# A kernel that plans its own order: norm weights copied inside SBUF for the last tokens, a two-regime transfer model, and a table of priority shifts

## The chip, the cores and the metric

The program runs on the 8 cores of one Trainium2 chip. Each core does one batch element, and no core talks to another. The metric is the device time of the slowest core, in microseconds. Before the change it was 1097.69 us (median of 3 runs).

## The reference, cut to what matters

One layer of a decoder: 16 meta tokens and 2048 tokens of width 1024 per core. A LayerNorm is applied first. Two attention branches (latent attention "MLA" and forgetting attention "FoX") follow, then gates, a merge, a second norm, a gated feed-forward with a short convolution, and a third norm.

```python
h = layer_norm(concat([meta, x]), ln_emb_g, ln_emb_b)           # 2064 tokens
m = hybrid_mixer(h, ...)                                        # two attentions, gates, merge
h = layer_norm(ALPHA * h + m, ln_mix_g, ln_mix_b)
f = conv_glu_ffn(h, ...)
h = layer_norm(ALPHA * h + f, ln_ffn_g, ln_ffn_b)
```

2064 tokens are 16 tiles of 128 and a rest of 16. The kernel spreads the rest over all partitions: four blocks of 32 rows, each with 256 of the 1024 columns. So the weights of the norms are needed in that form too.

## The kernel before

The kernel does not fix its order by hand. Its Python code records every operation as an item. A list scheduler (called the planner below) then simulates all engines with a table of durations. At each moment it starts, on each engine, the ready item of the lowest priority number. The resulting order of each engine is emitted; semaphores, not the planned times, make each operation wait for what it needs. The part that models a transfer:

```python
    RATE = 250.0                                    # bytes per ns
    LAND = {"sp": 2000.0, "pool": 2300.0}           # ns from the last byte to the semaphore
    ...
    def _prio(self, e, prio):
        b = prio if prio is not None else self.base.get(e, self.base.get("", 0.0))
        return b * 1e6 + len(self.items)
    ...
            if it.dma is not None:
                ...
                bus[0] = max(st + (1450.0 if e == "sp" else 1900.0), bus[0]) + it.bytes / self.RATE + 20.0
                end = bus[0] + self.LAND[e]
```

The loads for the last 16 tokens, called twice: in the first stage near 124 us, and before the second norm near 638 us.

```python
        def short_load(q, xb, pk, after):
            p4 = pk[:, :].rearrange("p (a n) -> p a n", a=4)
            for j in range(4):
                J, C = slice(32 * j, 32 * j + 32), slice(256 * j, 256 * j + 256)
                K.dma(q, xb[J, 0:256], xm[L - 32:L, C], after=after)
                K.dma(q, p4[J, :, :], lnp[0:4, C].partition_broadcast(32), after=after)
            K.dma(q, xb[:, 512:640], d_rep, after=after)
            return p4
```

The first norm's weights are already in SBUF, copied to all 128 partitions (`GBe`).

```python
        wfk = at(136832, 8 * 512).rearrange("p (k n) -> p k n", k=8)      # FoX key weights
        GBe = at(136832, 2048, F32).rearrange("p (a n) -> p a n", a=2)    # first norm's weights
```

Background copies ("paced") turn the branch weights `w_c` and the feed-forward weights `w_u` into bf16, HBM to HBM. The planner issues them from 50 us on, one after another, where its model of the queue has room. Many operands are transposed by DMA, SBUF to SBUF (`flip`), not by TensorE. The SBUF tensor is one array, so the profile names these transfers and the copies that the change adds both `SB<-SB`; the operation (DMA_TRANSPOSE or DMA_DIRECT2D) tells them apart where it is shown.

The softmax here doesn't subtract the row's maximum and nothing guards it: scores larger than these inputs give would overflow.

## Time and profile before

The page of the slowest core (core 2), busy time by engine and the chain that ended last. Columns of the first line: busy us, share of the span, instructions.

```profile
span 1095.9 us, 25665 instructions; the slowest of 8 cores (1089.0 to 1095.9 us)
...
PE 1061.2 (97%) x8230; PEld 602.7 (55%) x8316; DVE 744.7 (68%) x1674; ACT 619.9 (57%) x1362; POOL 178.9 (16%) x258
...
PE 88%; DMA 3%; issue 2%; ACT 2%; DVE 2%; POOL 1%; SPq 0%; DVEq 0%; POOLq 0%; ACTq 0%
```

TensorE (PE) is busy 97% of the time and is 88% of the chain, so what can be gained lies in TensorE's gaps and in work that is only filler: the kernel issues 200 dummy matmuls that fill TensorE's waits, nearly all before 50 us. The spans of the cores, with granted clock:

```profile
core 1: 1089.0 us, clock 0.995
core 2: 1095.9 us, clock 0.993
...
core 5: 1089.6 us, clock 0.993
...
die 0 (median of its cores): 1093.3 us, clock 0.994
die 1 (median of its cores): 1091.0 us, clock 0.994
```

The cores differ by 7 us at almost equal clocks, with the same program.

### The profile page before, as it was taken

How to read it: one execution, taken by the hardware profiler on the slowest of the kernel's cores; microseconds unless marked ns; L12 is line 12 of the kernel's file. 1: busy time of each engine (PE TensorE's matmuls, PEld its weight loads, DVE VectorE, ACT ScalarE, POOL GpSimd, SP SyncE). 2: the span in 40 equal slices, each digit the busy share in tenths (PEclk: the TensorE clock that was granted, in tenths of full speed). 3: DMA queues.
4: the chain of work that ended last, by engine and by line, in shares of the span. 5: the costliest groups of instructions: out<-in, count | busy, mean ns of one | idle time of the engine just before them, and what ended most of it. 6: DMA issues, size and time to landing. Idle time of an engine off the chain costs nothing.

```text
span 1095.9 us, 25665 instructions; the slowest of 8 cores (1089.0 to 1095.9 us)
## 1 busy us (share of the span) xinstructions
PE 1061.2 (97%) x8230; PEld 602.7 (55%) x8316; DVE 744.7 (68%) x1674; ACT 619.9 (57%) x1362; POOL 178.9 (16%) x258
## 2 busy tenths in 40 slices
PE   9999889999999999999999999999999999999995
PEld 6655556667454555565555566554456664444443
DVE  3899866764566676766668887656576765667754
ACT  5789879999778888887873254431034431023300
POOL 5434221121111220302111111101100000110010
PEclk9999999999999999999999999999999999999998
DMA  8858865754677797886989386962242232234301
GB/s 174 206 106 137 146 76 78 137 81 62 156 160 174 123 226 215 148 250 128 226 213 281 98 239 158 257 162 96 99 154 97 97 105 73 112 127 151 107 20 58
DMA packets 86867, 156.54 MB, mean 143 GB/s; under 512 B 39073, under 2 KB 43121, under 8 KB 86737
## 3 DMA queue, kind: packets, MB, share of 16 engines
q1 hardware_dynamic: 70066, 123.78, 38.4%
q0 software_dynamic: 16672, 31.11, 21.3%
q8 instruction: 72, 1.18, 0.5%
q14 instruction: 57, 0.47, 0.2%
HBM read 160.38 MB, written 34.67 MB: 178 GB/s over the span
## 4 chain that ended last, share of the span: by engine, by line
PE 88%; DMA 3%; issue 2%; ACT 2%; DVE 2%; POOL 1%; SPq 0%; DVEq 0%; POOLq 0%; ACTq 0%
PE PS L187 88%; ACT SB L187 2%; DVE SB L187 2%; DMA SB<-SB 2%; DMA SB<-scr_c 1%; POOL SB L187 1%; SPq L190 0%; ACT L187 0%; DVEq L226 0%; POOLq L226 0%; DVEq L245 0%; POOL scr_c L190 0%; POOL SB L190 0%; ACTq L245 0%; SPq L245 0%
## 5 line engine op out<-in xcount | busy, mean ns | idle before, releaser
L187 PE MATMUL PS<-SB 128*128 128x65 bf16 (+11 forms) x8230 | 1061.2, 291 | 22.5 <-DVE SB L187 6.7
L187 PEld LDWEIGHTS PS<-SB 128*128 128x128 bf16 (+2 forms) x8316 | 602.7, 98 | 480.7 <-issue 88.4
L187 ACT ACTIVATE SB<-PS,SB 128x384 bf16<-128x384 f32 (+9 forms) x611 | 315.3, 582 | 250.8 <-PE PS L187 243.9
L187 ACT ACTIVATE SB<-PS 128x384 bf16<-128x384 f32 (+11 forms) x547 | 215.3, 537 | 28.5 <-PE PS L187 24.5
L187 DVE SCALAR_TENSOR_TENSOR SB<-SB 128x1024 f32<-128x1024 f32 (+7 forms) x188 | 177.4, 948 | 14.6 <-POOL SB L187 7.1
L187 ACT ACTIVATE SB<-SB 128x384 f32<-128x384 f32 (+4 forms) x153 | 97.7, 645 | 141.4 <-DVE SB L187 141.1
L187 DVE SCALAR_TENSOR_TENSOR SB<-SB,PS 128x512 f32<-128x512 f32 (+3 forms) x146 | 90.2, 620 | 118.2 <-PE PS L187 93.7
L187 DVE SCALAR_TENSOR_TENSOR SB<-PS,SB 128x384 f32<-128x384 f32 (+1 forms) x220 | 141.0, 642 | 31.9 <-ACT SB L187 23.1
L187 POOL TENSOR_TENSOR SB<-SB 128x1 f32<-128x1 f32 (+1 forms) x67 | 81.8, 1222 | 434.1 <-DVE SB L187 433.6
L187 DVE TENSOR_TENSOR SB<-PS,SB 128x384 bf16<-128x384 f32 (+10 forms) x229 | 108.6, 480 | 61.1 <-ACT SB L187 53.7
L187 DVE TENSOR_TENSOR SB<-SB 128x128 bf16<-128x128 bf16 (+7 forms) x353 | 84.7, 268 | 31.2 <-ACT SB L187 23.7
L190 POOL DMA_DIRECT2D scr_u<-w_u x88 | 44.5, 506 | 266.9 <-ACT SB L187 261.7
L187 DVE CAST SB<-PS 128x512 bf16<-128x512 f32 (+5 forms) x85 | 50.6, 599 | 23.1 <-PE PS L187 18.5
L187 DVE BATCH_NORM_STATS2 SB<-SB 128x6 f32<-128x512 f32 (+1 forms) x85 | 56.9, 675 | 4.6
L187 DVE COPY SB<-SB 32x384 bf16<-32x384 bf16 (+2 forms) x80 | 19.7, 260 | 14.1 <-PE PS L187 12.5
L190 POOL DMA_DIRECT2D scr_c<-w_c x32 | 16.6, 520 | 64.6 <-ACT SB L187 62.7
L187 DVE COPY SB<-PS 128x2 f32<-128x2 f32 (+9 forms) x66 | 19.7, 306 | 8.1 <-PE PS L187 7.7
L190 POOL DMA_DIRECT2D SB<-w_dn x22 | 11.9, 541 | 78.4 <-ACT SB L187 78.4
L187 DVE TENSOR_SCALAR SB<-SB 128x1 f32<-128x1 f32 (+2 forms) x68 | 10.3, 152 | 18.7 <-ACT SB L187 15.9
L187 DVE RECIPROCAL SB<-PS 128x3 f32<-128x3 f32 (+3 forms) x84 | 14.1, 173 | 12.6 <-PE PS L187 11.2
L187 DVE TENSOR_SCALAR SB<-PS,SB 128x128 bf16<-128x128 f32 (+1 forms) x21 | 9.5, 461 | 1.4 <-POOL SB L187 1.0
L187 DVE BATCH_NORM_AGGREGATE SB<-SB 128x2 f32<-128x12 f32 (+2 forms) x43 | 8.6, 203 | 2.4
(20 smaller groups left out, 38.9 us busy)
## 6 DMA issues: line engine op xcount, KB each, us to landing
SB<-scr_u SPq DMA_DIRECT2D x66, 512.0 KB, 3.9
SB<-scr_c SPq DMA_DIRECT2D x80, 384.0 KB, 5.3
SB<-xm SPq DMA_DIRECT2D x31, 512.0 KB, 6.8
scr_u<-w_u POOLq DMA_DIRECT2D x88, 128.0 KB, 4.0
scr_h<-SB SPq DMA_DIRECT2D x16, 512.0 KB, 4.9
SB<-scr_h SPq DMA_DIRECT2D x16, 512.0 KB, 3.5
out<-SB SPq DMA_DIRECT2D x15, 512.0 KB, 2.6
scr_c<-w_c POOLq DMA_DIRECT2D x32, 192.0 KB, 4.2
```

Source lines behind the costliest of these rows:

```text
L187: return self._add(eng, lambda e: getattr(e, name)(*args, **kw), rd, wr)
L190: return self._add(eng, lambda e: e.dma_start(out=out, in_=in_, **kw), [in_], [out], dma_key=key, after=after)
```

## The change

Its intent: replace eight broadcast reads from HBM by copies inside SBUF; give the planner a second regime of transfer times from 56 us on, with faster rate and earlier landing; and shift the priorities of each of 215 parts of the recording by a table, one number for TensorE and one for all other engines. The numbers look like the result of a search.

```diff
+    LATER = 56.0
+    RATE2 = 290.0
+    LAND2 = {"sp": 1000.0, "pool": 1200.0}
...
     def _prio(self, e, prio):
         b = prio if prio is not None else self.base.get(e, self.base.get("", 0.0))
-        return b * 1e6 + len(self.items)
+        k = self.part + (self.line != self.of or self.part < 0)
+        return b * 1e6 + len(self.items) + (RAISED[k][e != "pe"] if k < len(RAISED) else 0)
...
-                bus[0] = max(st + (1450.0 if e == "sp" else 1900.0), bus[0]) + it.bytes / self.RATE + 20.0
-                end = bus[0] + self.LAND[e]
+                late = st >= 1e3 * self.LATER
+                bus[0] = max(st + (1450.0 if e == "sp" else 1900.0), bus[0]) + it.bytes / (self.RATE2 if late else self.RATE) + 20.0
+                end = bus[0] + (self.LAND2 if late else self.LAND)[e]
...
+RAISED = ((-13118, -36714), (-8248, 20214), (9486, 14943), (22487, 38948),   ... 215 pairs, cut
...
-        def short_load(q, xb, pk, after):
+        def short_load(q, xb, pk, after, gains):
...
-                K.dma(q, p4[J, :, :], lnp[0:4, C].partition_broadcast(32), after=after)
+                for a, g in enumerate(gains):
+                    K.dma(q, p4[J, 2 * a:2 * a + 2, :], g[J, :, C], after=after)
...                                  # first stage: gains = (GBe,); second norm: gains = (GB0, GBm)
```

(`self.part` counts the parts as items are recorded; those lines are cut.)

## The prediction

> **What bounds it now.** The table of busy time by engine gives TensorE 97% (1061 of 1095.9 us); the chain of waits is 88% matmuls. From 740 to about 1075 us (feed-forward) TensorE has no gap: one 512-column matmul every 216 to 219 ns. [...]
>
> A new order can recover part of the dummies' time (DVE is already busy 16 to 19.8 of every 20 us from 20 to 120 us), part of the larger gaps, and what the slowest core loses beyond the others. Cores span 1089.0 to 1095.9 us at equal clocks; core 2 also waits for SBUF-to-SBUF transposes (8.15 us on its chain to 136 us, 6.7 us to 159 us) and one load near 608 us, costing TensorE 0.7 + 2.0 + 2.7 + 1.3 us.
>
> **What the change does.**
> 1. Copies for the last tile. Removed: 8 broadcast reads of 128 KB, 6.1 us (first norm, issued at 124 us) to 9.3 us (at 638 us) to landing. Added: 4 + 8 copies of 64 KB inside SBUF, four more issues at 0.43 us of SyncE. None is in this trace; estimate 3 to 6 us to landing, from 6.1 us for the 64 KB constant load. At 638 us TensorE is full: worth 0. At 124 us the four issues (2.4 us) stand in the chain just before a transpose; their count stays: 0 to 1.5 us gained.
> 2. Transfer model: from 56 us the planner believes in landings about 1 us earlier and rate 290 instead of 250. The 512 KB loads land in 3.9 us by the DMA list, near that; transposes take 5.4 us, later. Only order changes: -1 to +3 us.
> 3. Priority shifts, mean 0.02, at most 0.1, against 0.005 per token tile: four tiles of reordering on average. Matmul work is unchanged. Filled gaps and earlier real work: 4 to 14 us gained, before about 300 us.
>
> **Prediction.** 1089 us, range 1079 to 1098. Chances: faster by over 2% 0.05, within 2% 0.92, slower by over 2% 0.03.
>
> **What would show it.** Right: matmul counts by form unchanged; the feed-forward stretch as long as before (within 1 us) but starting 5 to 12 us earlier; gaps over 200 ns before 300 us shrink; the score bursts keep their short gaps; the broadcast loads leave the DMA list, and TensorE waits for none of the new copies. Wrong on item 1: undoing the copies alone costs over 2 us. Wrong on item 2: undoing the model alone is faster, or TensorE gains waits on loads after 56 us.
>
> **What would make it wrong.** The shifts mix attention with dense filler so well that the short burst gaps vanish (then 1070 or below), or real work replaces most dummies; or the optimistic model makes loads late, several waits of 2 us each (about 1100); or the slowest core's DMA luck moves by its 7 us.

My sum for core 1 came to about 1075 us up to the last matmul (1029 of matmuls, 46 of gaps), and about 9 us after it. Its matmul times, and with them the split of the gaps, rested on a spacing that was not measured here, so "1070 or below" in the last paragraph is only an estimate of mine; the 9 us are not shown either. What the trace of core 1 shows: the matmuls run from 1.5 to 1076.8 us, and 12.2 us follow. From start to start a 512-column matmul takes 215 to 216 ns. The 200 dummies (256 columns) take 109 ns each in the median, about 22 us in all, and start before 44 us. The short gaps of the score bursts are seen in the 64-row pairs of 384 columns: after a pair the next one starts 169 to 170 ns later, but what follows the last pair of a burst 255 ns later (44 times). The larger gaps, over 200 ns and before 300 us, come to 8.3 to 12.0 us (six cores). The forecast: the middles of its three items (0.75 gained, 1 lost, 9 gained) take 1097.7 us to 1089.

## More of the kernel before

Core 1 has a record without missing matmuls, so I read details from it. What TensorE waited for on core 1 from 60 to 165 us (us in total, times, longest):

```profile
PE PS L187 <- ACT SB L187: 2.2, 6, 1.0
PE PS L187 <- DVE SB L187: 1.2, 2, 0.9
PE PS L187 <- DMA SB<-SB: 0.4, 2, 0.2
```

Stretches of core 1 (busy time and count for PE, PEld, DVE, ACT, POOL; then granted clock, DMA share, GB/s):

```profile
60.00:165.00 105.00, 100.70 (x958) 59.12 (x956) 96.67 (x300) 94.03 (x254) 33.42 (x48) 1.00 0.67 120
...
300.00:520.00 220.00, 219.69 (x2041) 119.63 (x2039) 148.63 (x309) 176.39 (x363) 41.70 (x64) 1.00 0.82 181
520.00:640.00 120.00, 119.64 (x961) 69.29 (x959) 89.76 (x172) 66.95 (x123) 16.95 (x21) 1.00 0.78 212
```

From 60 to 165 us the engines are closest to each other: PE 100.7, DVE 96.7 and ACT 94.0 of 105 us. From 300 us on TensorE is full.

## The result and the profile after

The changed kernel takes 1108.46 us (median of 4 runs) against 1097.1 us for the kernel before in the same session. The ratio is 1.0103, with a 95% interval of 1.0085 to 1.0121. Ratios here are the mean time of one kernel's runs over that of the other's in the same rounds, so they are not quite the ratio of the medians. Executions in which one die ran at a lower clock are left out of the means. The change is slower by 1.0%: still within 2%, but in the wrong direction and outside the range I gave.

The page of the slowest core after:

```profile
span 1106.0 us, 25703 instructions; the slowest of 8 cores (1094.0 to 1106.0 us)
...
PE 1063.4 (96%) x8229; PEld 602.5 (54%) x8316; DVE 742.4 (67%) x1670; ACT 622.4 (56%) x1366; POOL 173.2 (16%) x258
...
PE 80%; DMA 7%; DVE 4%; issue 3%; ACT 3%; POOL 1%; SPq 0%; DVEq 0%; POOLq 0%; ACTq 0%
```

TensorE does the same work; more of the chain is now transfers (7%, it was 3%) and other engines. The spans:

```profile
core 1: 1102.0 us, clock 0.990
core 2: 1106.0 us, clock 0.992
...
core 5: 1097.7 us, clock 0.995
...
core 7: 1094.0 us, clock 0.993
die 0 (median of its cores): 1102.8 us, clock 0.992
die 1 (median of its cores): 1099.8 us, clock 0.993
```

Every core is later than in the profile of before (by 1.7 to 13.0 us), and they spread over 12 us where they had spread over 7. The waits of TensorE on core 1 from 60 to 165 us, and core 1's stretches:

```profile
PE PS L187 <- DMA SB<-SB: 6.5, 5, 2.9
PE PS L187 <- ACT SB L187: 2.0, 3, 1.4
PE PS L187 <- DVE SB L187: 1.9, 2, 1.5
```

```profile
60.00:165.00 105.00, 94.33 (x876) 54.51 (x875) 87.32 (x272) 86.95 (x235) 29.50 (x46) 0.97 0.69 118
...
300.00:520.00 220.00, 217.60 (x2039) 118.23 (x2038) 142.49 (x305) 175.89 (x363) 43.79 (x73) 1.00 0.83 182
520.00:640.00 120.00, 118.04 (x964) 66.47 (x962) 91.45 (x181) 66.28 (x125) 10.87 (x8) 1.00 0.64 186
```

TensorE's wait for SBUF-to-SBUF transfers went from 0.4 to 6.5 us. TensorE is busy 6.4 us less between 60 and 165 us, and even its granted clock fell, from 1.00 to 0.97. On the six cores with complete records this wait was 0.3 to 3.0 us before and 3.7 to 7.7 us after. The largest gap, on core 0, in the timeline (start us, us, engine, line, operation; in brackets the idle time before it and what ended it), then the same core in stretches of 4 us:

```profile
126.51 2.52 PE L187 MATMUL PS<-SB 128*128 128x512 bf16 x26 [0.26 <-DMA SB<-SB]
127.45 1.20 SPq L190 DMA_TRANSPOSE SB<-SB  x1
...
133.37 3.21 PE L187 MATMUL PS<-SB 128*128 128x72 bf16 x30 [4.33 <-DMA SB<-SB]
```

```profile
125.00:129.00 4.00, 3.75 (x38) 2.14 (x36) 3.67 (x10) 3.90 (x11) 1.30 (x2) 1.00 1.08 90
129.00:133.00 4.00, 0.03 (x1) 0.00 (x0) 1.92 (x6) 1.19 (x4) 0.55 (x1) 1.00 1.15 138
133.00:137.00 4.00, 3.63 (x32) 2.39 (x33) 1.08 (x5) 0.55 (x2) 0.55 (x1) 0.57 1.13 259
```

TensorE stands still for 4.33 us, until transposed tokens land: the matmuls that then start (72 columns) read the transposed first norm. The chain of this core names the transfer (start us, us, what). It is the transpose issued before the one in the timeline above:

```profile
124.24 8.99 DMA SB<-SB
```

The planner had given this transpose 4.09 us; on the eight cores it took 7.2 to 9.0 us. Right after the gap the granted clock is 0.57. The clock records show a window of 3.4 us at half clock at 133.4 us on this core. Windows of 3.4 or 6.8 us at half clock lie between 130 and 155 us on cores 0, 1, 2, 3 and 7 after; before, one core had one between 60 and 170 us (core 2, at 159.5 us). (At the start, from 7.7 to 14.0 us, six cores have one before and seven after.) On the cores with complete records each of these windows began within 1.3 us of the end of a gap of TensorE: 4.33 us (core 0), 2.95 (core 1), 3.84 and 2.08 (core 3) and 2.73 (core 7). But core 6 had none after a gap of 3.66 us, so the length of the gap alone does not decide it; what does is not shown. So a late transfer can cost more than its wait. The same 65 matmuls after that gap show how much, on core 6 (no half clock), core 7 (3.4 us of it) and core 1 (6.8 us of it):

```profile
136.52 6.31 PE L187 MATMUL PS<-SB 128*128 128x72 bf16 x65 [3.66 <-DMA SB<-SB]
```

```profile
131.77 7.99 PE L187 MATMUL PS<-SB 128*128 128x72 bf16 x65 [2.73 <-DMA SB<-SB]
```

```profile
135.53 9.04 PE L187 MATMUL PS<-SB 128*128 128x72 bf16 x65 [2.95 <-DMA SB<-SB]
```

They take 6.31, 7.99 and 9.04 us: 1.7 and 2.7 us more.

The timeline shows one thing more: the issue of a transpose keeps SyncE busy for 1.20 us. Over all cores it is 1.2 us in the median, against 0.3 us for the other transfers (0.3 to 0.7 for 90% of them) and 0.6 us for the new copies.

The DMA lists of core 1 between 60 and 165 us, before and then after (count, KB each, median us from issue to landing):

```profile
SB<-xm SPq DMA_DIRECT2D x5, 512.0 KB, 4.9
...
SB<-lnp SPq DMA_DIRECT2D x4, 128.0 KB, 5.0
...
SB<-SB SPq DMA_TRANSPOSE x16, 4.6
```

```profile
SB<-xm SPq DMA_DIRECT2D x5, 512.0 KB, 6.3
...
SB<-SB SPq DMA_TRANSPOSE x16, 5.0
SB<-SB SPq DMA_DIRECT2D x4, 64.0 KB, 5.6
```

The transposes take longer in the median (5.0 against 4.6 us), the token loads 6.3 against 4.9 us, and the new copies land no sooner than the broadcasts did (5.6 against 5.0 us).

### Plan against chip

The planner's own start time of each matmul can be written out, and the n-th matmul of the plan is taken for the n-th of the trace (the six complete records of each kernel show their 8316 matmuls in the same order of forms). I call "slip" the start on the chip less the planned start, both counted from the first matmul. Planner spans are no measurements; the slip is what the measurement adds. Medians over the cores with complete records, at four points of planned time:

```
                       planner us   slip at 60    160    540    700 us
before                   1084.4        -0.4       3.0    7.9   -1.6
changed                  1071.2         0.2      11.4   19.2   20.6
```

This shows three things. The planner promised 13.2 us. First, the changed order loses 7.8 us more than the kernel before between 60 and 160 us, where it waits for transposes (8.4 us with what it lost earlier). Second, some 3 us more go between 160 and 540 us. Third, the kernel before gains 9.5 us on its own plan between 540 and 700 us, and the changed one loses 1.4. That last part is no fault of the changed order. The plan of the kernel before holds 10.9 us of idle TensorE between 520 and 640 us, waiting for loads; the plan of the changed kernel holds 1.1. On the chip core 1 of the kernel before was busy 119.64 of these 120 us (table of before). So 9.8 of the 13.2 us promised were the removal of waits that existed only in the plan.

How late single transfers were, by matching each landing on the chip to the planned one, all 8 cores:

```
                                     planned   measured mean   90th percentile   over 1 us late
before   transposes     56 to 170 us   5.59         4.70             6.8                8%
changed  transposes     56 to 170 us   4.27         4.96             6.9               41%
before   token loads   300 to 550 us   9.15         6.59             8.0                1%
changed  token loads   300 to 550 us   6.83         7.00             9.1               28%
```

The new times are near the measured means, and that is the trouble as I read it: 41% of the transposes and 28% of the token loads then land over 1 us later than planned, and what waits for one of them starts late. On core 0 the 72-column matmuls started 0.14 us after the 8.99 us transpose had landed (133.23 us); the transpose issued before it had landed 6.9 us earlier.

### The profile page after: what moved, and what is told of

It reads as the page before. It is cut to its first block, busy times and chain, and to the rows that moved or that the text cites. A ratio compares the mean times of both kernels' runs of the same rounds, so it can differ in the third digit from the quotient of the medians.

```text
span 1106.0 us, 25703 instructions; the slowest of 8 cores (1094.0 to 1106.0 us)
## 1 busy us (share of the span) xinstructions
PE 1063.4 (96%) x8229; PEld 602.5 (54%) x8316; DVE 742.4 (67%) x1670; ACT 622.4 (56%) x1366; POOL 173.2 (16%) x258
## 4 chain that ended last, share of the span: by engine, by line
PE 80%; DMA 7%; DVE 4%; issue 3%; ACT 3%; POOL 1%; SPq 0%; DVEq 0%; POOLq 0%; ACTq 0%
PE PS L187 80%; DMA SB<-xm 4%; DVE SB L187 4%; ACT SB L187 3%; DMA SB<-SB 3%; POOL SB L187 0%; DMA scr_h<-SB 0%; SPq L190 0%; POOL SB L190 0%; ACT L187 0%; DVEq L226 0%; DVEq L245 0%; POOLq L226 0%; ACTq L245 0%; SPq L245 0%
## 5 line engine op out<-in xcount | busy, mean ns | idle before, releaser
L187 PE MATMUL PS<-SB 128*128 128x384 bf16 (+9 forms) x8229 | 1063.4, 291 | 30.6 <-DVE SB L187 12.2
L187 PEld LDWEIGHTS PS<-SB 128*128 128x128 bf16 (+1 forms) x8316 | 602.5, 98 | 491.2 <-issue 100.6
L187 ACT ACTIVATE SB<-PS,SB 128x384 bf16<-128x384 f32 (+9 forms) x618 | 318.9, 580 | 252.4 <-PE PS L187 246.8
L187 POOL TENSOR_TENSOR SB<-SB 128x1 f32<-128x1 f32 (+1 forms) x67 | 76.5, 1145 | 540.7 <-DVE SB L187 538.6
L187 DVE TENSOR_TENSOR SB<-PS,SB 128x384 bf16<-128x384 f32 (+9 forms) x229 | 108.3, 480 | 65.9 <-ACT SB L187 56.8
L187 DVE TENSOR_TENSOR SB<-SB 128x128 bf16<-128x128 bf16 (+9 forms) x353 | 84.0, 268 | 25.9 <-ACT SB L187 18.9
L187 DVE CAST SB<-PS 128x384 bf16<-128x384 f32 (+5 forms) x86 | 50.8, 595 | 22.6 <-PE PS L187 21.5
L190 POOL DMA_DIRECT2D SB<-w_dn x22 | 11.9, 543 | 73.4 <-ACT SB L187 73.2
L187 POOL MEMSET SB<- 128x1152 bf16 (+8 forms) x16 | 8.6, 638 | 0.0
```

The lines of the kernel that those rows point to most:

```text
L187: return self._add(eng, lambda e: getattr(e, name)(*args, **kw), rd, wr)
L190: return self._add(eng, lambda e: e.dma_start(out=out, in_=in_, **kw), [in_], [out], dma_key=key, after=after)
```

## The experiments

Theory "late landings": the planner now believes that transfers after 56 us land at about their mean time. Its order has no room for the late ones, and TensorE waits. Rivals: the small copies hold up the transposes; or the shifts by themselves make a bad order; or any change of a tuned planner makes it worse. Each kernel ran beside the kernel before on the same chip. Chips differed: the kernel before took 1096.5 to 1101.9 us in the median, so ratios are compared, not times. All results were correct by the comparison with the reference.

"The queue" stands in these texts for all transfers of a core together. In the trace they run in two: the paced copies are issued by POOL (q0), the transposes and token loads by SyncE (q1), and from 115 to 160 us on core 1 of the kernel before the packets of q0 took 48.1% of the time of the 16 DMA engines, those of q1 31.8%.

One thing disturbs the slips. In the profiles of e5 to e8 and e13 to e15 the clock records show stretches of 4 to 15 us at 13/16 of the clock (0.8125), on two neighbouring cores at a time; the other profiles have none (before and after: 0.50 or 1.00 only). They cost a core up to 8.5 us (in e15's profile cores 6 and 7 have mean clocks of 0.985 and 0.986, the others 0.990 to 0.997). The kernel before was slowed in those calls too: its mean granted clock was 0.989 beside e5 to e8 and 0.992 beside e13 to e15, against 0.994 in the other calls. So the ratios compare like with like, but the slips of these runs hold time that the slip of the kernel before (from another call) does not. Where it matters, the slip without that time is given as well.

### Taking the three parts out (e1 to e4)

```diff
 e1_no_copies     -  for a, g in enumerate(gains): K.dma(q, p4[J, 2*a:2*a+2, :], g[J, :, C], after=after)
                  +  K.dma(q, p4[J, :, :], lnp[0:4, C].partition_broadcast(32), after=after)
 e2_no_regime     -  LATER = 56.0
                  +  LATER = 1e9
 e3_no_shifts     -  (RAISED[k][e != "pe"] if k < len(RAISED) else 0)
                  +  (RAISED[k][e != "pe"] if False else 0)
 e4_regime_only      e1 and e3 together
```

> The change with the norm weights of the last 16 tokens again broadcast from HBM; regime and shifts kept. The instruction order stays that of the changed kernel but for small local differences, and the planner's own span is 1071.3 us, as with the copies (1071.2). Theory 'late landings' (the planner believes landings after 56 us that the chip doesn't give, so that waits appear from 70 to 160 us): no change, 1105 to 1111 us. Rival 'copies' (the four small SBUF-to-SBUF copies near 130 us hold up the transposes): 3 to 7 us faster than the changed kernel, and the gaps of TensorE between 120 and 160 us at least halve.

Measured: 1112.36 us, ratio 1.0136 (1.0103 to 1.0170). No faster than the changed kernel, so the copies are not the cause.

> Copies and shifts kept, the planner's one-regime transfer times restored for the whole run. The planner now says 1097.7 us for its own order. Theory 'late landings': the chip follows the plan as it did for the kernel before (planner 1084.4, chip 1097), so planner + about 13 us: 1108 to 1113 us, but TensorE's slip against the plan by the end is under 8 us on the median core, where it was 19 to 23 in the changed kernel. Rival 'shifts are good in themselves and only the transfer model spoils them': under 1095 us.

Measured: 1113.65 us, ratio 1.0144 (1.0121 to 1.0167). The slip at 700 us is 2.9 us: the chip follows this plan as it followed that of the kernel before. But the plan itself is 13 us longer. The shifts fit the two-regime planner and make things worse under the other, so "good in themselves" falls.

> Copies and two regimes kept, shifts off. The planner says 1088.8 us. Theory 'late landings' in its plain form (two regimes are too optimistic for any order): slip of 19 us or more again, chip at planner + 25 to 37: 1114 to 1126 us. Variant 'the shifts were fitted to the model' (they only leave out the slack that other orders have by accident): slip well below 19 us, chip at planner + 13 to 20: 1102 to 1109 us. Rival 'the shifts alone make the order bad': 1093 to 1099 us, as before the change.

Measured: 1118.07 us, ratio 1.0192 (1.0172 to 1.0211). The median slip at 700 us is 14.7 us, less than the 19 that the plain theory asked for, but the time is planner + 29 as it said. "The shifts alone make the order bad" falls: without them it is slower still.

> The kernel before with the two-regime transfer model alone; no copies, no shifts. The planner says 1088.7 us (1084.4 with one regime). Theory 'late landings', plain: 1110 us or more. 'Fitted shifts': 1100 to 1108 us. 'Shifts alone are bad': 1095 to 1100 us.

Measured: 1121.02 us, ratio 1.0209 (1.0176 to 1.0241), slip 14.9 us. The transfer model alone, which the prediction had put at -1 to +3 us, costs 2.1%, about 23 us. Its waits on core 1 from 60 to 165 us look like those of the changed kernel:

```profile
PE PS L187 <- DMA SB<-SB: 5.7, 4, 2.0
PE PS L187 <- ACT SB L187: 2.4, 7, 0.5
```

### Where in time the regime hurts (e5, e6)

```diff
-                late = st >= 1e3 * self.LATER
+                late = 1e3 * self.LATER <= st < 1e3 * self.UNTIL       # e5: 170 to the end; e6: 56 to 170
```

> The kernel before with the two-regime transfer model alone, the second regime starting at 170 us instead of 56; no copies, no shifts. The planner says 1084.7 us; its order agrees with that of the kernel before until 170 us. Theory 'too optimistic from 60 to 170 us, where transposes, token loads and background copies share the queue': 1096 to 1103 us, and TensorE's slip against the plan until 160 us is that of the kernel before (up to 5 us). Rival 'too optimistic everywhere': 1110 us or more, with new waits on token loads after 300 us.

Measured: 1114.88 us, ratio 1.0119 (1.0093 to 1.0146). The expectation "1096 to 1103" was wrong. The slip at 160 us is 5.0 us, near that of before, but it grows to 11.9 at 540 and 14.8 at 700 us (without the time at 13/16 of the clock: 3.4, 10.4 and 10.5; the kernel before had 3.0, 7.9 and -1.6). So the late part hurts by itself. This plan too holds 10.9 us of idle TensorE between 520 and 640 us, but now some of these waits are real: from 540 to 660 us TensorE waits 3.3 us for branch weights and 2.2 us for VectorE on core 1, where the list of the kernel before shows no wait.

> The complement: the second regime believed only from 56 to 170 us, the first again after it. The planner says 1092.4 us. Theory 'too optimistic from 60 to 170 us': slip of 6 to 12 us by 160 us, time 1108 to 1116 us. Rival 'the harm comes after 170 us': planner + 13, about 1105 us, with a slip under 5 us at 160 us.

Measured: 1115.83 us, ratio 1.0119 (1.0098 to 1.0141); slip 8.2 us at 160, 6.2 at 700 us (4.9 without the time at 13/16 of the clock); its plan is 8.0 us longer. The two halves together (1.2% and 1.2%) make up about what e4 costs. The theory holds for both, and my narrowing of it to the early part does not.

### Less traffic beside the same order (e7, e8, e10)

If late landings open the gaps, the gaps should close in the same order when the queue is emptier. e7 keeps the order of the changed kernel but issues none of the paced copies of rank 1 and 4 (branch and feed-forward weights) before 170 us. They follow in the later places of that queue, and the last places take two copies each. e8 does the same to the kernel before. e10 takes the doubled places from 200 us on instead; there (200 to 260 us) the DMA share of core 1 of the changed kernel is 0.67, and from 400 to 480 us it is 0.96.

```diff
     def replay(self):
+        self.postpone(170.0)    # paced copies: places after 170 us only; the first ones first,
+                                # two in each of the last places (e7, e8) or from 200 us on (e10)
```

> The changed kernel with its instruction order kept on every engine except for one thing: the background copies that turn the branch weights into bf16 (HBM to HBM) are not issued before 170 us, and the whole queue of background copies follows in the later places. Theory 'late landings': with the queue free the transposes land near their planned time, TensorE's slip at 160 us falls from 11 to 14 us to under 6 us, and the time falls by 5 to 9 us, to 1100 to 1104 us. Rival 'the order itself is bad, whatever the transfers do': unchanged at 1106 to 1112 us.

> The control: the same move of the background copies in the kernel before. It has slack there (TensorE waited 0.4 us for transposes from 60 to 165 us on core 1), so both theories expect little: 1094 to 1098 us; the slowest core may lose the 5 us it waited for transposes.

> e7 again, its flaw mended: the background copies moved out of 60 to 170 us are now made up two at a time from 200 to 260 us, where the queue is emptier, not from 400 to 480. Order of everything else as in the changed kernel. Theory 'late landings': TensorE's slip at 160 us 2 to 9 us on the cores with full records, where the changed kernel had 11 to 14; time 3 to 8 us below the changed kernel of the same call. Rival 'order bad in itself': no change in slip or time.

Measured: e7 1.0248 (1.0230 to 1.0266), e8 1.0064 (1.0022 to 1.0106), e10 1.0183 (1.0165 to 1.0202). All are slower, so the expected times were wrong. The slips say why. At 160 us e7 has 5.8 and e10 8.4 us (up to 170 us of the plan they are the same program), where the changed kernel had 11.4, and 11.9 when it ran again (e12). The control e8 has 3.2, the kernel before 3.0. The transpose that took 7.2 to 9.0 us in the changed kernel (planned 4.09) takes 2.7 or 2.8 us on every core of e7 and e10, with the small copies still beside it. So it was late because of the paced copies, and 3 to 6 of the 8.4 us of early slip go with them. TensorE's wait for SBUF-to-SBUF transfers on core 1 of e7 from 60 to 165 us is 0.9 us, not 6.5; but core 1 is the best one (six cores: 0.9 to 4.6 us in e7, 3.3 to 6.5 in e10, 3.7 to 7.7 in the changed kernel):

```profile
PE PS L187 <- DVE SB L187: 1.9, 2, 1.5
PE PS L187 <- ACT SB L187: 1.8, 2, 1.4
PE PS L187 <- DMA SB<-SB: 0.9, 1, 0.9
```

What is left of the early slip is mostly not late landing: the transposes planned from 56 to 170 us land in 3.5 us (e7) and 3.6 us (e10) in the mean, faster than the planned 4.27, and 6% and 8% of them are over 1 us late. On the median core the transpose planned at 126.5 us is issued 4.4 us (e7) and 5.5 us (e10) behind the plan, when TensorE itself is only 1.8 and 3.2 us behind. What holds up that issue is not shown.

Then the moved copies did their own damage where they were doubled. On core 1 e7's slip grows from 5.9 us at 400 us to 30.8 at 500 us; e10's grows from 13.7 to 35.4 us between 270 and 330 us, with waits of 5.0 and 10.5 us. The loads of branch weights (384 KB) show it: they take 17.9 us to landing in the median between 260 and 340 us in e10, where the changed kernel has 5.5, and 12.8 us between 400 and 500 us in e7, where it has 6.0. I had not allowed for that. These runs show what made much of the early slip; as a repair they fail.

### The copies by themselves (e11, e12, e13, e17, e18)

e11 keeps every instruction of the changed kernel and only reads the 12 small transfers from HBM again; e12 is the changed kernel beside it.

```diff
-            K.dma(q, p4[J, 2*a:2*a+2, :], g[J, :, C], after=after)
+            K.dma(q, p4[J, 2*a:2*a+2, :], g[J, :, C], after=after).swap = lnp[2*a:2*a+2, C].partition_broadcast(32)
```

> The changed kernel, order and count of all instructions kept exactly; only the source of its 12 small copies is put back to the broadcast from HBM (64 KB each). By the theory that the copies are not the cause: within 2 us of the changed kernel of the same call, either way. Rival 'SBUF-to-SBUF copies hold up the transposes': 3 us faster or more.

> The changed kernel itself, as the reference for e10 and e11 on the same chip: ratio 1.008 to 1.013.

Measured: e11 1.0142 (1.0112 to 1.0171), e12 1.0111 (1.0091 to 1.0131). The copies are no slower than the broadcasts; they may be up to a few us faster, which these intervals do not settle.

e13, e17 and e18 add the copies to the kernel before. e13 and e17 hold its order: in the emission each broadcast is replaced by its copies. In e17 the first load of the FoX key weights (`wfk`) also moves behind the four early copies. e18 plans anew.

```diff
 e13     -  the broadcast                     +  the same place: copy from GBe, or copies from GB0 and GBm
 e17     as e13, and the first wfk load stands after the fourth early copy
 e18     the change's short_load alone: LATER = 1e9, shifts off
```

> The kernel before with its plan and the order of its instructions kept; only, where a broadcast load of the last 16 tokens' norm weights stood, the copy or copies inside SBUF stand instead (the four near 124 us one for one; near 638 us two for each, the second on a semaphore of its own). By my prediction's item 1: 0 to 1.5 us faster, ratio 0.998 to 1.001. Rival 'copies are harmful': ratio 1.003 or more.

> e13 with its fault mended. In e13 the four early copies stood after the first load of the forgetting-branch key weights, which lies in the same memory as the first norm's weights, so that they waited for that load and read the wrong bytes. Here that load stands after the four copies (as it does in the changed kernel); otherwise the order of the kernel before. If the copies themselves cost nothing and e13's loss was that wait: ratio 0.998 to 1.003. If holding the norm's memory longer and the copies cost something in this order: 1.003 or more.

> The kernel before with the copies alone, planned anew with the one-regime transfer model. The planner says 1094.3 us (1084.4 without copies; its w_fk loads start at 130 instead of 122 us because the copies hold that memory). Drawn transfers: 1087.7 against 1082.9. By the planner: ratio 1.009. By the timing under drawn transfers: 1.003 to 1.006. If neither matters: 1.000.

Measured: e13 1.0045 (1.0032 to 1.0058); its slip at 160 us was 8.3 us. This run is faulty: `GBe` and `wfk` share memory, the copies stood after the first `wfk` load, so they waited for it (124.2 to 130.4 us on core 1's chain) and read wrong bytes for the last 16 tokens. The comparison still passed, which I do not count as correct; the run says nothing about copies. Mended, e17 takes 1098.35 us, ratio 0.9979 (0.9961 to 0.9998): the copies alone, in the held order, gain about 2 us (0.2 to 4.3), a little over the 0 to 1.5 us of the prediction's item 1. On core 1 they land in 2.0 us (median, 60 to 165 us), and TensorE waits 0.3 us for SBUF-to-SBUF transfers:

```profile
SB<-SB SPq DMA_DIRECT2D x4, 64.0 KB, 2.0
```

```profile
PE PS L187 <- ACT SB L187: 2.3, 7, 1.0
...
PE PS L187 <- DMA SB<-SB: 0.3, 1, 0.3
```

e18: 1108.17 us, ratio 1.0072 (1.0051 to 1.0092). The same copies planned anew cost 0.7%. The slip is 2.4 us at 700 us; the plan is 9.9 us longer. Its `wfk` loads start at 130 us in the plan, not 122, since the copies hold their memory longer. Whether that wait or the reshuffling makes the longer plan, these runs do not tell.

### Other shifts (e9, e14, e15)

I searched tables of shifts of the same form myself, for the kernel before, with one regime and without the copies: e9 for the planner's span, e14 and e15 for the mean span of the order when timed again with transfer times drawn from those measured in the first runs.

```diff
-RAISED = ((-13118, -36714), ...      # and LATER = 1e9, broadcasts as before
+RAISED = ( ... 215 other pairs ... )
```

> The kernel before (one regime, no copies) with another table of priority shifts of the same form, found by a random search of my own against the one-regime planner; the planner says 1075.3 us (1084.4 without shifts). If the orders of the kernel before and of this one are timed again with transfer times drawn at random from those measured in the runs so far, the means are 1083.7 and 1079.0 us. Theory 'shifts help where the transfer times behind them leave room for late landings': 1088 to 1094 us on a chip where the kernel before takes 1097, ratio 0.992 to 0.998. Rival 'any shifts that please the planner are fitted to it and the chip gives nothing back': ratio 1.00 or above.

> The kernel before with a third table of shifts, searched not for the planner's span but for the mean over six drawings of transfer times from those measured on the chip, with the order timed again under each. The planner says 1080.0 us for it (1075.3 for e9's), the timing under drawn transfers (24 new drawings) 1075.3 us against 1078.4 for e9's order, 1082.9 for the kernel before, 1092.9 for the changed kernel. Theory 'an order is worth what it does under the spread of landings, not under single times': faster than the kernel before, ratio 0.993 to 0.997. Rival 'what is left is not transfers' (e9 gave 0.999 where the same timing promised 0.996): ratio 0.998 to 1.002.

> A second, independent result of the same search as e14: planner 1082.7 us, 1076.5 us under drawn transfers. The same expectations: 0.994 to 0.998 by the theory, 0.998 to 1.002 by the rival. If e14 and e15 agree within 0.3% the result is not the luck of one order.

Measured: e9 0.9993 (0.9975 to 1.0011), e14 1.0021 (0.9997 to 1.0044), e15 0.9997 (0.9979 to 1.0016). None is faster than the kernel before. e9's planned gain of 9.1 us went the way described above: its plan holds 2.8 us of idle TensorE from 520 to 640 us (before 10.9), and its slip between 540 and 700 us falls by 1.5 us where that of the kernel before falls by 9.5. Of the planned orders whose drawn timing is on record, e4's came last (1104 us), as on the chip, but the transfers were drawn from those very runs, and the search with them did not find a better kernel. So part of "an order is worth what it does under the spread" stays unproven: it explains bad orders and did not yield a good one.

### The mirror image (e16)

```diff
-    RATE2 = 290.0
-    LAND2 = {"sp": 1000.0, "pool": 1200.0}
+    RATE2 = 250.0
+    LAND2 = {"sp": 3000.0, "pool": 3300.0}      # no copies, no shifts
```

> The mirror image of e4: no copies, no shifts, and from 56 us on landings that the planner believes 1 us LATER than the kernel before did (3.0 and 3.3 us after the last byte instead of 2.0 and 2.3; rate 250), where e4 believed them 1 us earlier. The planner says 1093.7 us, 5 us worse than e4's 1088.7 and 9 worse than the kernel before. With transfers drawn from the measured ones the order takes 1084.0 us (kernel before 1082.9, e4 1104). Theory 'the planner's belief about landings must cover their spread': ratio 0.998 to 1.006, and 15 us or more faster than e4's 1.021, against the planner's own ranking. Rival 'e4 is slow because any change of the transfer model reshuffles a tuned order': ratio 1.012 or more.

Measured: 1108.05 us, ratio 1.0082 (1.0047 to 1.0117). It lies between the two expectations. The planner held this order for 5 us worse than e4's; on the chip it is about 1.3% better (1.0209 / 1.0082), some 14 us. The slip at 700 us is 1.1 us, against 14.9. So belief in earlier landings costs slip, and belief in later ones does not. (The timing with drawn transfers had said 1.001; that was too low.) But the 9 us of longer plan are paid in full, so "any change of a tuned planner costs" has a share as well. TensorE's waits on core 1 from 60 to 165 us:

```profile
PE PS L187 <- ACT SB L187: 2.6, 6, 1.2
PE PS L187 <- DMA SB<-SB: 2.3, 1, 2.3
```

### All together

If plan and slip are the whole story, a kernel's time against the kernel before should be the change of the planner's span plus the change of the slip. Us; "measured" is the ratio less 1, times 1100:

```
                      planner   change    slip at 700   change     sum   measured
e1  no copies          1071.3    -13.1        22.1       +23.7    +10.6     +15.0
e2  no regime          1097.7    +13.3         2.9        +4.5    +17.8     +15.8
e3  no shifts          1088.8     +4.4        14.7       +16.3    +20.7     +21.1
e4  regime only        1088.7     +4.3        14.9       +16.5    +20.8     +23.0
e5  regime from 170    1084.7     +0.3        14.8       +16.4    +16.7     +13.1
e6  regime 56 to 170   1092.4     +8.0         6.2        +7.8    +15.8     +13.1
e9  own shifts         1075.3     -9.1         9.3       +10.9     +1.8      -0.8
e12 changed, again     1071.2    -13.2        21.1       +22.7     +9.5     +12.2
e14 spread a           1080.0     -4.4         4.6        +6.2     +1.8      +2.3
e15 spread b           1082.7     -1.7         4.6        +6.2     +4.5      -0.3
e16 later landings     1093.7     +9.3         1.1        +2.7    +12.0      +9.0
e18 copies, planned    1094.3     +9.9         2.4        +4.0    +13.9      +7.9
```

The sums are within about 6 us of the measured differences. The median core of one profiled execution stands beside the slowest core of several, so more is not to be expected. Without the time at 13/16 of the clock the sums of e5, e6, e14 and e15 are 12.4, 14.5, 1.0 and 0.9 us, nearer to the measured ones. Left out are the changed kernel itself (sum +9.0, measured +11.3), e11 (+13.3, +15.6), e17 (+1.0, -2.3), the faulty e13, and the three kernels whose queue was changed after planning; of these e8 fits worst (+14.0, or +10.7 without that time, against +7.0). The table is bookkeeping: the slip is measured on these very runs, so it shows where the time goes, and the single experiments must show why. Every order planned with the earlier landings until the end has a slip of 14.7 to 22.1 us (e5's is 10.5 without the time at 13/16). Every one planned without them, but e9's, has one under 5.

## Why the prediction was wrong, point by point

- **What bounds the kernel: right.** TensorE's matmul counts by form are unchanged, and from the first 386-column matmul to the last matmul core 1 takes 472.5 us before and 471.5 after. But that stretch starts at 616.7 us instead of 602.5 (core 1), or 612.5 instead of 607.5 (core 0), counted from the first matmul: later, not "5 to 12 us earlier".
- **Item 1, the copies: right only while the order is held.** "0 to 1.5 us gained"; in the held order e17 measures about 2 us. But the planner makes a new order around the copies, and with that they cost 0.7%, about 8 us (e18); the item had no term for it. "Estimate 3 to 6 us to landing": 5.6 us in the changed kernel on core 1, 2.0 us in e17. I had missed that `GBe` shares memory with `wfk`, so the copies delay a weight load: its first issue is at 134.6 us in the changed kernel and at 128.1 in e1 (medians over cores, counted from the first matmul). No loss from that shows there: the last of these loads lands at 154.3 and 154.4 us.
- **Item 2, the transfer model: the step that failed.** "Only order changes: -1 to +3 us." Alone it measures about 23 us (e4), of which 4 are in the plan and 16 are slip. I compared the new times with the 3.9 us landing of the 512 KB loads, a median over 66 loads that mostly run after 640 us, where nobody waits. I noted that transposes take "5.4 us, later" and did not ask what the order does with that. A median says nothing about the late half. In the changed kernel the transpose behind the longest gap took 7.2 to 9.0 us, where its plan had 4.09. Of the two tests that I had named for this item, one came out: TensorE gained waits on transfers after 56 us (0.4 to 6.5 us on core 1). The other, "undoing the model alone is faster", did not (e2 1.0144, e12 1.0111), because the shifts fit the new model.
- **Item 3, the shifts: the size was right under the new model only.** "4 to 14 us gained"; e3 against the changed kernel gives 0.9%, about 9 us. With the one-regime planner the same shifts cost 0.7% (e18 1.0072, e2 1.0144). They cannot be costed apart from the model that they were fitted to. Added one after another, the copies planned anew cost about 8 us (e18), the new model 13 more (e3 against e18), and the shifts give back about 10 (the changed kernel against e3). I had written 0 to 1.5 gained, -1 to +3, and 4 to 14 gained. The parts do not add up in every order: with the shifts on, the regime gains 0.3% (e2 against e12); with them off, it costs 1.2% with the copies (e18, e3) and 2.1% without (e4).
- **"Filled gaps and earlier real work":** of the 13.2 us planned, 9.8 were waits between 520 and 640 us that only the old plan had. And the gaps over 200 ns before 300 us, which I expected to shrink, grew from 8.3 to 12.0 us to 12.4 to 18.2 us (six cores). I could not know the plan, but the table of before showed TensorE full there, and I should have asked how the new order could gain anything the chip had not already.
- **"What would make it wrong"** named it: late loads, "several waits of 2 us each (about 1100)". I gave it too little weight, and left out the clock: five cores had windows of 3.4 or 6.8 us at half clock near the ends of such waits.

What stays open: what holds up the issue of the later transposes when the queue is empty (e7, e10); how much of e4's and e16's loss is a reshuffled tuned order; and whether the copies' 2 us survive beyond one chip and four runs. e17 is the fastest kernel here, by 0.2%, which is hardly outside its interval.

## What to carry to other kernels

A schedule searched against a model is only as good as the model's worst terms. Before trusting its gain, compare planned with measured start times on a trace of the kernel before, and see whether the promised us come out of waits that the chip really has. If a planner gives transfers about their mean time, an order that fills every gap has no room for the late ones (in the changed kernel 41% of the transposes from 56 to 170 us were over 1 us late), and gaps of TensorE can cost clock as well: here windows at half clock came with gaps of 2.1 to 4.3 us, though not with every one. That more room makes a faster kernel is not shown here: e16 gave it, kept its slip small, and lost 0.8% by a longer plan. When an addition reads a buffer for longer than before, look up who gets that memory next.
